# Twelve modulation tiles of layer 0 moved from VectorE row sums to TensorE, and the remaining row sums dealt out anew over the two down projections

## The chip, the cores and the metric

The kernel runs on one core of a Trainium2 chip. The metric is device time in microseconds (us) of one execution; the time given is the median of three. TensorE is PE in the rows, VectorE DVE, ScalarE ACT, GpSimd POOL; SyncE's queue (SP) issues most of the loads.

## The reference

Two layers of a diffusion backbone over 256 latent and 256 context tokens, width 1024. What matters here is the modulation: six vectors per layer are computed from the conditioning `c` and, for the context, from `c_ctx`, and they scale, shift and gate everything else.

```python
silu_c, silu_cc = silu(c), silu(c_ctx)
xc = ctx
for layer in range(2):
    mod   = silu_c  @ w_mod[layer] + b_mod[layer]      # 1024 -> 6 * 1024
    mod_c = silu_cc @ w_mod[layer] + b_mod[layer]
    sh1, sc1, g1, sh2, sc2, g2 = split(mod, 6)         # and the same for mod_c
    h, hc = rms_norm(x, n1) * (1 + sc1) + sh1, ...
    y, yc = mixer(h, hc)      # layer 0: neighbourhood attention + gated linear attention
    x  = x + g1 * y           # layer 1: retention, latent output only
    h2 = rms_norm(x, n2) * (1 + sc2) + sh2
    x  = x + g2 * conv_ffn(h2, up, down)
    ...                       # the context xc likewise, in layer 0
return rms_norm(x)
```

## The kernel before

All 512 tokens are held feature by feature (X, eight blocks of 128 features by 512 tokens). Every weight product is made of three fp32r products (helper `mm3`, lines 297 to 299): high part by high part, high by low, low by high. A weight piece of 128 x 1024 (a down projection's pieces are 768 and 640 wide) is loaded into one of the four slots of the ring `raw` (line 240, on SP's queue), copied rounded by ScalarE into `WH` (line 261), and the remainder is formed into `WL` by VectorE for a job's first piece (line 265) and by GpSimd for its second (line 263). `WH` and `WL` have four slots, two jobs' worth.

The work is a list of **jobs** (two output blocks of an up or input projection; one block of a down projection). `pieces` is the list of loads in the order of the jobs; piece n goes into raw slot n mod 4, and a slot is loaded again when the piece in it has been read. `before` puts extra pieces ahead of a job's weights. There are two kinds:

- **A modulation piece on TensorE** (`mods`, `use_mod`, lines 435 on, products at line 302): a quarter of the 1024 input features by 512 columns of `w_mod`. Eight small fp32 products, 128 x 128 by 128 x 32, each into a quarter of a PSUM bank; each shows as two records. Four pieces make one block of four tiles (128 modulation values each); the bank is held over the four, and the first of them is put off as long as no bank is to be had. Then `mod_post` transposes the bank on VectorE (line 467), adds the bias (478) and, for scales, makes `amod` (485).
- **A row sum on VectorE** (`row_sums`, `use_row`, line 453): one tile, 128 rows of 1024 weights, multiplied with the broadcast conditioning and summed along the row by one tensor_tensor_reduce; a second pass for the context where the tile needs it. Scales take one more small instruction per pass (459).

Blocks 0 to 3 (tiles 0 to 15) are computed on TensorE at the very start. In the mixer stage ("mix": two value jobs of the linear attention, six jobs of the neighbourhood attention, two gate jobs) the kernel before has twelve TensorE pieces (tiles 16 to 27) and twelve row sums (tiles 28 to 39, `ROWS0`, two passes each). The other 56 row sums (tiles 40 to 47 of layer 0 with two passes, then 48 tiles of layer 1, the first 16 of them with two passes) lie in the feed-forward part of layer 0: one per job from the third of the first 13 up jobs (stage up0), two per job in the eight jobs of the first down projection (down0a), two per job in the nine further up jobs (up0b), two per job and one at the last in six jobs of the second (down0b).

A row sum needs the broadcast conditioning `cb` in SBUF. `open_rows` (line 1446) passes it through Silu on ScalarE (1448); it is called ahead of the mixer stage (1491) and again, with a fresh load, ahead of the output projection (1532). The two buffers of the first call, 2048 and 512 columns, are held until the mixer's scope is closed.

Beside the jobs run side tasks that are advanced in turn: the linear attention (`gla_gen`, `gla_head`: scans on VectorE at lines 787 and 851, small fp32 products) and four `na_pair` tasks, which begin by taking 3072 columns of scratch. With the first `cb` buffers in place 648 columns are free until linear attention heads give up theirs.

The order on each engine is not the program's: the framework arranges the instructions by a plan of times (`_TC = {"schedule_with_timeline_sim": True}`), and each engine then runs its list strictly in that order. Stages as read from the profile: start to 58 us, mixer jobs and side tasks 58 to 284, output projection 284 to 332, up0 332 to 476, down0a 476 to 539, up0b 539 to 652, down0b and its tail 652 to 715, layer 1 from 715.

Of the kernel before, what the change touches and what calls it, by code (L numbers as in the profile page):

```python
# [47 lines left out]
HID1 = 13056  # L48
NA0 = 4 * 2560
ROWS0 = tuple(range(28, 40))  # L50
RAWS = 4
WSL = 4
GLA_PAUSE = 14
# [75 lines left out]
def kernel(ctx: ExitStack, tc: tile.TileContext, I: dict, out: bass.AP):  # L129
    nc = tc.nc  # L130
# [4 lines left out]
    X = const.tile([128, KT, N2], F32, name="x")  # L135
    raw = const.tile([128, RAWS, 1024], F32, name="raw")
    WH = const.tile([128, WSL, 1024], F32R, name="wh")
# [30 lines left out]
    def buf(n, high=False, where="m"):  # L168
        b = (small if where == "s" else scope[where]).get(n, high)
        assert b is not None, (n, where)  # L170
        return b
# [65 lines left out]
    def try_load(upto=10000):  # L237
        while st["load"] < min(upto, len(pieces)) and st["load"] - st["piece"] < RAWS:
            src = pieces[st["load"]][0]
            nc.sync.dma_start(raw[:, st["load"] % RAWS, 0:src.shape[1]], src)  # L240
            st["load"] += 1

    def prep_next():
# [3 lines left out]
        src, use, arg = pieces[i]  # L247
        if not use(raw[:, i % RAWS, 0:src.shape[1]], *arg):
            return False
# [390 lines left out]
    def before(src, use, *arg):  # L640

        k = len(jobs)
        aux.setdefault(k, []).append((src, lambda *a: st["cur"] >= k - 1 and use(*a), arg))

    m_todo = deque()
    r_todo = deque()

    def mods(n):
        for _ in range(min(n, len(m_todo))):
            layer, c, q = m_todo.popleft()  # L650
            before(I["w_mod"][layer, c, q // 2][:, 1024 * (q % 2):1024 * (q % 2) + 1024], use_mod, layer, c, q)

    def row_sums(n):
        for _ in range(min(n, len(r_todo))):
            i, layer, t, both = r_todo.popleft()
            before(I["w_row"][i], use_row, layer, t, both)
# [595 lines left out]
    if True:  # L1252
# [11 lines left out]
        def mark(name):  # L1264
            seg[name] = len(jobs)

        def win(i, run):
            return W(I["w_in"][i], 2048, run)
# [8 lines left out]


        mark("mix")
        m_todo.extend((0, c, q) for c in range(4, 10) if 4 * c not in ROWS0 for q in range(4))  # L1280
        r_todo.extend((i, *r) for i, r in enumerate(_row_tiles()))
        mix = [win(8, tm_run(post_tm("gv", 0, 0))), win(9, tm_run(post_tm("gv", 256, 1)))]
        for hf in range(2):
            mix.append(win(hf, fm_run(8, [2 * hf, 2 * hf + 1], h_all, 512, post_naq, 4)))
# [4 lines left out]
        for i, j in enumerate(mix):  # L1289
            if i == 2:  # L1290
                mark("na")
            if i == 8:
                mark("gr")
            mods(-(-(24 - len(ROWS0)) * (i + 1) // 10) + (24 - len(ROWS0)) * i // -10)
            row_sums(-(-len(ROWS0) * (i + 1) // 10) + len(ROWS0) * i // -10)
            ja(j)

        def o_rhs(kt):
# [30 lines left out]
            ja(up_job(0, i, 512, S_[1]))  # L1329
        mark("down0a")  # L1330
        for m in range(8):
            row_sums(2)
            ja(down_job(0, 0, m, fm_run(HALF, [m], hid_rhs(0, 0, 512), 512, resid_post(0, 5, None, True), 4)))
        mark("up0b")
        for i in range(13, NFF):
# [1 line left out]
            ja(up_job(0, i, 512, S_[1]))  # L1337
        mark("down0b")
        for m in range(6):
            row_sums(2 if m < 5 else 100)  # L1340
            ja(down_job(0, 1, m, fm_run(HALF, [m], hid_rhs(HALF, 0, 512), 512, resid_post(0, 5, S_[2], True), 4)))
        mark("down0t")
        jl_d = [down_job(0, 1, m, None) for m in (6, 7)]
# [61 lines left out]
        nc.scalar.activation(ccs[:, :, :], ccs[:, :, :], AF.Silu)  # L1405
        sqrt_next()
        st["cur"] = 0
        dump = buf(512, True)
        G["msk"] = buf(256)
        m0 = []  # L1410

# [34 lines left out]
        def open_rows(cb, dump):  # L1446
            with after_h():
                nc.scalar.activation(cb.ap, cb.ap, AF.Silu)
            G["cb"], G["dump"] = cb, dump
# [13 lines left out]
        with tc.manual_schedule(engines={mybir.EngineType.PE}):  # L1463
            mod_pair(0)
            load_mod(6)
            load_mod(7)
            nc.sync.dma_start(cst[:, 0:C_SEL], I["cst"][:, 0:C_SEL])
            nc.sync.dma_start(G["msk"].ap.bitcast(I32), I["msk"])
            with tc.issue_after(first_h(0)):
                assert prep_next()  # L1470
            with after_h():
                assert prep_next()
            first_h(1)
            with after_h():
                assert prep_next() and prep_next()
            for c in range(4):
                first_mm(c, range(5))
                if c < 3:
                    mod_pair(c + 1)
                    if c == 1:  # L1480
                        row_bufs = [buf(2048, True), dump]
                        nc.sync.dma_start(row_bufs[0].ap, I["cb"])
                    first_h(2 * c + 2)
                    first_h(2 * c + 3)
                first_mm(c, range(5, 8))
# [2 lines left out]
        piece_done(jgq, 2)  # L1488
        for i in range(4):
            posts.append((post_gqk("k2", None) if i < 2 else post_gqk("q2", 0.125))(i % 2, gb[i]))  # L1490
        open_rows(*row_bufs)
        small.next = 0
        G["ws1"] = buf(2048, where="s")
        G["gpk"] = Sub(G["ws1"], 0, 1280)
# [35 lines left out]
        row_bufs = [buf(2048, True), buf(512)]  # L1530
# [150 lines left out]
def _row_tiles():  # L1681

    return [(0, t, True) for t in ROWS0 + tuple(range(40, 48))] + [(1, t, t < 16) for t in range(48)]

# [141 lines left out]
```

## Time and profile before

| | us |
|---|---|
| Three executions | 1213.65, 1217.60, 1224.94 |
| Median | 1217.6 |
| Profiled execution, own time | 1224.02 |
| Its span in the profile | 1222.2 |
| TensorE busy | 1165.3 (95%) |
| VectorE busy | 819.5 (67%) |
| TensorE's mean granted clock | 0.977 of full |

Busy is the time in which an engine has an instruction in hand; a product at half clock counts as busy too. The granted clock has two levels here, 1.0 (2.4 GHz) and 0.5 (1.2 GHz), so that a stretch of length L with mean clock m had (1 - m) x L of full-speed time taken away.

### The profile page before, as it was taken

How to read it: one execution, taken by the hardware profiler on the slowest of the kernel's cores; microseconds unless marked ns; L12 is line 12 of the kernel's file. 1: busy time of each engine (PE TensorE's matmuls, PEld its weight loads, DVE VectorE, ACT ScalarE, POOL GpSimd, SP SyncE). 2: the span in 40 equal slices, each digit the busy share in tenths (PEclk: the TensorE clock that was granted, in tenths of full speed). 3: DMA queues.
4: the chain of work that ended last, by engine and by line, in shares of the span. 5: the costliest groups of instructions: out<-in, count | busy, mean ns of one | idle time of the engine just before them, and what ended most of it. 6: DMA issues, size and time to landing. Idle time of an engine off the chain costs nothing.

```text
span 1222.2 us, 19879 instructions
## 1 busy us (share of the span) xinstructions
PE 1165.3 (95%) x7846; PEld 1023.8 (84%) x7846; DVE 819.5 (67%) x1344; ACT 547.5 (45%) x933; POOL 462.6 (38%) x326
## 2 busy tenths in 40 slices
PE   4999999989999999989899999999999999999997
PEld 3677866767898888867688889889999999999996
DVE  4498886464498889966865256647977736877532
ACT  4452344264463443212344364534555546666542
POOL 2124234232432322121212339954643354443342
PEclk8999988999999999989999989999999999999998
DMA  9653554213334445677643323322223553655562
GB/s 371 234 180 125 184 172 153 86 52 108 104 119 149 143 149 176 208 253 251 228 150 106 109 92 121 105 71 85 70 70 128 183 190 127 210 181 180 153 182 91
DMA packets 52365, 184.79 MB, mean 151 GB/s; under 512 B 5824, under 2 KB 6208, under 8 KB 50736
## 3 DMA queue, kind: packets, MB, share of 16 engines
q1 hardware_dynamic: 50256, 175.20, 43.5%
q0 software_dynamic: 1728, 7.80, 1.9%
q8 instruction: 61, 1.00, 0.3%
q10 hardware_dynamic: 288, 0.52, 0.1%
q14 instruction: 32, 0.26, 0.1%
HBM read 182.46 MB, written 1.05 MB: 150 GB/s over the span
## 4 chain that ended last, share of the span: by engine, by line
PE 69%; DVE 14%; DMA 6%; POOL 5%; issue 3%; ACT 2%; SPq 0%; DVEq 0%; ACTq 0%; POOLq 0%
PE bank L297 20%; PE bank L299 20%; PE bank L298 20%; PE bank L302 9%; DVE space L453 5%; DMA raw<-in_w_row_dram 5%; DVE wl L265 2%; POOL wl L263 1%; DVE space_r L1055 1%; PE bank L983 1%; POOL space L1151 1%; POOL space L1152 1%; DMA x<-in_xT_dram 1%; DVE space L1023 1%; DVE amod L459 1%
## 5 line engine op out<-in xcount | busy, mean ns | idle before, releaser
L263 POOL TENSOR_TENSOR wl<-raw,wh 128x1024 fp32r<-128x1024 f32 (+1 forms) x124 | 284.9, 2297 | 563.5 <-ACT wh L261 553.1
L299 PE MATMUL bank<-hh,wl 128*128 128x256 f32 (+1 forms) x1200 | 402.8, 336 | 13.8 <-DVE wl L265 11.1
L297 PE MATMUL bank<-hh,wh 128*128 128x256 f32 (+1 forms) x1200 | 403.5, 337 | 8.6 <-DVE space L989 3.5
L298 PE MATMUL bank<-hl,wh 128*128 128x256 f32 (+1 forms) x1200 | 402.6, 336 | 5.1 <-DVE hl L547 5.1
L261 ACT CAST wh<-raw 128x1024 fp32r<-128x1024 f32 (+1 forms) x248 | 241.9, 978 | 256.5 <-PE bank L298 125.3
L299 PEld LDWEIGHTS bank<-hh,wl 128*128 128x128 f32 x1200 | 230.4, 192 | 39.1 <-DVE wl L265 12.8
L297 PEld LDWEIGHTS bank<-hh,wh 128*128 128x128 f32 x1200 | 230.7, 192 | 36.2 <-ACT hh L545 4.0
L298 PEld LDWEIGHTS bank<-hl,wh 128*128 128x128 f32 x1200 | 230.5, 192 | 29.1 <-DVE hl L547 6.0
L265 DVE TENSOR_TENSOR wl<-raw,wh 128x1024 fp32r<-128x1024 f32 (+1 forms) x124 | 153.2, 1235 | 101.6 <-ACT wh L261 99.2
L453 DVE CUSTOM_DVE_ANT_0 space<-raw,space,vec 128x1024 bf16<-128x1024 f32 x104 | 155.0, 1490 | 39.4 <-DMA raw<-in_w_row_dram 35.1
L299 PE MATMUL bank<-space_r,wl 128*128 128x256 f32 (+1 forms) x374 | 123.6, 330 | 1.0 <-DVE wl L265 1.0
L298 PE MATMUL bank<-space_r,wh 128*128 128x256 f32 (+1 forms) x374 | 122.9, 329 | 0.0
L297 PE MATMUL bank<-space_r,wh 128*128 128x256 f32 (+1 forms) x374 | 122.3, 327 | 0.0
L297 PE MATMUL bank<-wh,hh 128*128 128x256 f32 x384 | 109.8, 287 | 0.3 <-ACT wh L261 0.3
L299 PE MATMUL bank<-wh,hl 128*128 128x256 f32 x384 | 108.8, 284 | 0.0
L298 PE MATMUL bank<-wl,hh 128*128 128x256 f32 x384 | 108.7, 283 | 0.0
L299 PEld LDWEIGHTS bank<-space_r,wl 128*128 128x128 f32 x374 | 70.3, 188 | 8.4 <-DVE wl L265 1.7
L1023 DVE SCALAR_TENSOR_TENSOR space<-bank,vec,space 128x510 f32<-128x510 f32 (+1 forms) x88 | 53.6, 610 | 34.7 <-ACT space L1019 34.6
L297 PEld LDWEIGHTS bank<-space_r,wh 128*128 128x128 f32 x374 | 70.7, 189 | 7.3 <-issue 0.4
L298 PEld LDWEIGHTS bank<-space_r,wh 128*128 128x128 f32 x374 | 70.2, 188 | 7.4
L297 PEld LDWEIGHTS bank<-wh,hh 128*128 128x128 f32 x384 | 73.2, 191 | 2.9 <-issue 2.1
L298 PEld LDWEIGHTS bank<-wl,hh 128*128 128x128 f32 x384 | 73.4, 191 | 1.7 <-DVE space L683 0.8
(249 smaller groups left out, 1641.6 us busy)
## 6 DMA issues: line engine op xcount, KB each, us to landing
raw<-in_ffn_up_dram SPq DMA_DIRECT2D x88, 512.0 KB, 3.8
raw<-in_w_row_dram SPq DMA_DIRECT2D x68, 512.0 KB, 4.2
raw<-in_ret_in_dram SPq DMA_DIRECT2D x48, 512.0 KB, 3.6
raw<-in_w_in_dram SPq DMA_DIRECT2D x24, 512.0 KB, 4.7
raw<-in_ffn_down_dram SPq DMA_DIRECT2D x32, 384.0 KB, 3.2
raw<-in_ffn_down_dram SPq DMA_DIRECT2D x32, 320.0 KB, 2.9
space<-in_w_mod_dram SPq DMA_DIRECT2D x8, 1024.0 KB, 13.8
raw<-in_ret_out_dram SPq DMA_DIRECT2D x16, 512.0 KB, 3.8
```

Source lines behind the costliest of these rows:

```text
L261: nc.scalar.copy(WH[:, s, 0:n], src)
L263: nc.gpsimd.tensor_tensor(WL[:, s, 0:n], src, WH[:, s, 0:n].bitcast(F32), op=ALU.subtract)
L265: nc.vector.tensor_sub(WL[:, s, 0:n], src, WH[:, s, 0:n].bitcast(F32))
L297: nc.tensor.matmul(out_ap, lhsT=ah, rhs=bh, start=first, stop=False, skip_group_check=True)
L298: nc.tensor.matmul(out_ap, lhsT=ah, rhs=bl, start=False, stop=False, skip_group_check=True)
L299: st["pe"] = nc.tensor.matmul(out_ap, lhsT=al, rhs=bh, start=False, stop=last, skip_group_check=True).ins
L302: st["pe"] = nc.tensor.matmul(out_ap, lhsT=lhsT, rhs=rhs, start=start, stop=stop, skip_group_check=True).ins
L453: nc.vector.tensor_tensor_reduce(G["dump"].ap.bitcast(BF16), src, G["cb"].ap[:, 1024 * v:1024 * v + 1024], 1.0, vec[:, V_BMOD + 48 * layer ...
L459: nc.vector.scalar_tensor_tensor(out=amod[:, layer, s // 4, k, v:v + 1], in0=modt[:, layer, t, v:v + 1], scalar=1.0, in1=vec[:, g0:g0 + 1] ...
L983: nc.tensor.transpose(banks[bs[e]][:, u * 256 + qt * 128:u * 256 + qt * 128 + 128], gs[e][:, qt, u, :], ident)
L1023: nc.vector.scalar_tensor_tensor(out=yv[:, :, 1:256], in0=pv[:, :, 0:255], scalar=vec[:, w:w + 1], in1=yv[:, :, 1:256], op0=ALU.mult, op1= ...
L1055: nc.vector.tensor_sub(hl, yb.ap, hh.bitcast(F32))
```

## The change

The twelve row sums of the mixer stage are no longer made; blocks 7, 8 and 9 (tiles 28 to 39) join the TensorE pieces, 24 instead of 12 over the ten jobs, and the 24 extra loads of the stage stay 24, of 512 KB each. The first `open_rows`, its 1 MB load of `cb` and the two buffers fall away. The 56 other row sums stay, in the same order; in down0a there is one per job instead of two, in down0b three instead of two (and four instead of one at its sixth job). So eight row sums go from down0a to later jobs.

```diff
+SKIP = len(ROWS0)
...
-        m_todo.extend((0, c, q) for c in range(4, 10) if 4 * c not in ROWS0 for q in range(4))
-        r_todo.extend((i, *r) for i, r in enumerate(_row_tiles()))
+        m_todo.extend((0, c, q) for c in range(4, 10) for q in range(4))
+        r_todo.extend((i, *r) for i, r in enumerate(_row_tiles()) if i >= SKIP)
...
-            mods(-(-(24 - len(ROWS0)) * (i + 1) // 10) + (24 - len(ROWS0)) * i // -10)
-            row_sums(-(-len(ROWS0) * (i + 1) // 10) + len(ROWS0) * i // -10)
+            mods(24 * (i + 1) // 10 - 24 * i // 10)
...
         mark("down0a")
         for m in range(8):
-            row_sums(2)
+            row_sums(1)
...
         mark("down0b")
         for m in range(6):
-            row_sums(2 if m < 5 else 100)
+            row_sums(3 if m < 5 else 100)
...
-        dump = buf(512, True)
...
-                    if c == 1:
-                        row_bufs = [buf(2048, True), dump]
-                        nc.sync.dma_start(row_bufs[0].ap, I["cb"])
...
-        open_rows(*row_bufs)
```

## Rows read from the trace of the kernel before

**Rows 1.** The page's first part: busy time of each engine, share of the span, instructions.

```profile
PE 1165.3 (95%) x7846; PEld 1023.8 (84%) x7846; DVE 819.5 (67%) x1344; ACT 547.5 (45%) x933; POOL 462.6 (38%) x326
```

**Rows 2.** Busy time by stage: stretch, its length, then busy us (instructions) of PE, PEld, DVE, ACT and POOL, the granted clock, the DMA engines' share, GB/s.

```profile
58.00:190.00 132.00, 124.62 (x918) 96.54 (x916) 113.90 (x232) 53.60 (x104) 44.68 (x44) 0.95 0.49 162
190.00:284.00 94.00, 90.26 (x538) 67.59 (x536) 50.72 (x102) 41.13 (x95) 27.24 (x31) 0.95 0.25 83
...
476.00:539.00 63.00, 62.05 (x266) 49.43 (x266) 53.87 (x93) 13.40 (x18) 13.99 (x7) 1.00 0.69 216
539.00:652.00 113.00, 101.87 (x434) 82.47 (x433) 84.92 (x118) 39.02 (x52) 23.22 (x10) 0.97 0.61 202
652.00:715.00 63.00, 63.00 (x344) 53.25 (x344) 20.06 (x31) 22.32 (x31) 19.86 (x14) 1.00 0.33 101
```

**Rows 3.** The same view for line 453 alone (VectorE's row sums; each pass counts two instructions): stretch, length, DVE busy.

```profile
58.00:190.00 132.00, 33.86 (x48) 0.95 0.49 162
...
476.00:539.00 63.00, 33.90 (x50) 1.00 0.69 216
```

**Rows 4.** TensorE's timeline in the mixer stage, three rows at which it had waited for VectorE's scans: start us, us, instruction, and in brackets the idle time before it and what ended that.

```profile
92.17 0.66 PE L302 MATMUL bank<-cst,space 128*64 128x128 f32 x8 [1.24 <-DVE space L787]
...
114.42 0.50 PE L297 MATMUL bank<-hh,wh 128*128 128x512 f32 x1 [1.93 <-DVE x L851]
...
162.88 1.52 PE L302 MATMUL bank<-space_r 128*128 128x512 f32 x2 [1.95 <-DVE x L851]
```

**Rows 5.** The granted clock around five waits (columns as in rows 2).

```profile
112.00:120.00 8.00, 6.07 (x35) 4.24 (x34) 6.96 (x19) 0.89 (x2) 4.87 (x3) 0.79 0.15 38
160.00:174.00 14.00, 12.05 (x58) 7.60 (x57) 12.62 (x37) 1.78 (x5) 2.88 (x1) 0.63 0.59 189
187.00:198.00 11.00, 9.25 (x48) 6.68 (x48) 6.51 (x14) 4.42 (x14) 2.94 (x5) 0.69 0.75 236
258.00:266.00 8.00, 4.48 (x13) 3.53 (x13) 4.95 (x7) 6.24 (x18) 2.87 (x3) 0.79 0.42 131
539.00:550.00 11.00, 7.03 (x21) 5.29 (x20) 8.39 (x11) 2.10 (x2) 2.36 (x1) 0.69 0.72 236
```

**Rows 6.** TensorE's timeline in down0a and up0b: the rows at which it had waited for a weight's remainder.

```profile
531.88 0.50 PE L299 MATMUL bank<-space_r,wl 128*128 128x512 f32 x1 [0.95 <-DVE wl L265]
...
543.82 0.80 PE L299 MATMUL bank<-hh,wl 128*128 128x512 f32 x1 [3.97 <-DVE wl L265]
...
580.46 0.50 PE L299 MATMUL bank<-hh,wl 128*128 128x512 f32 x1 [1.47 <-DVE wl L265]
...
594.56 0.50 PE L299 MATMUL bank<-hh,wl 128*128 128x512 f32 x1 [2.93 <-DVE wl L265]
...
608.45 0.50 PE L299 MATMUL bank<-hh,wl 128*128 128x512 f32 x1 [2.71 <-DVE wl L265]
```

**Rows 7.** What that queue waited for between 476 and 620 us: total us, times, longest.

```profile
SPq L240 <- DVE modt L453: 62.6, 35, 4.3
SPq L240 <- DMA raw<-in_w_row_dram: 21.7, 15, 3.5
```

**Rows 8.** The queue that issues the loads, in a stretch of up0b: start us, us (of the group), load, count.

```profile
580.43 0.33 SPq L240 DMA_DIRECT2D raw<-in_ffn_up_dram  x1
585.18 2.26 SPq L240 DMA_DIRECT2D raw<-in_w_row_dram  x2
587.53 0.38 SPq L240 DMA_DIRECT2D raw<-in_ffn_up_dram  x1
589.89 3.23 SPq L240 DMA_DIRECT2D raw<-in_w_row_dram  x2
594.53 0.33 SPq L240 DMA_DIRECT2D raw<-in_ffn_up_dram  x1
```

**Rows 9.** The chain of waits ahead of 58 us, where two modulation pieces (x16) lie between products of 512 columns: start us, us.

```profile
44.11 0.57 PE bank L302 x16
44.68 0.43 PE bank L297
45.12 0.57 PE bank L302 x16
45.69 0.43 PE bank L298
46.12 0.23 PE bank L299
```

**Rows 10.** TensorE's timeline: a modulation piece on TensorE at which it waited, and the wait just before it.

```profile
189.42 0.66 PE L983 MATMUL bank<-cst,space 128*128 128x128 f32 x4 [1.53 <-DVE space_r L724]
...
190.41 1.08 PE L302 MATMUL bank<-raw,ccs 128*32 128x128 f32 x16 [0.22 <-DMA raw<-in_w_mod_dram]
```

**Rows 11.** Groups by line and shape: busy us, mean ns of one, idle before.

```profile
L453 DVE CUSTOM_DVE_ANT_0 space<-raw,space,vec 128x1024 bf16<-128x1024 f32 x104 | 155.0, 1490 | 39.4 <-DMA raw<-in_w_row_dram 35.1 <-ACT space L1448 3.8
```

**Rows 12.** One VectorE instruction of each `mod_post`: times in ns (least, median, most).

```profile
L467 DVE STREAM_TRANSPOSE small<-bank x7: 313/317/318, 19.3 to 191.6; 128x128 f32<-128x128 f32 x7
```

**Rows 13.** TensorE's timeline: the third long wait of the mixer stage.

```profile
261.55 0.52 PE L297 MATMUL bank<-hh,wh 128*128 128x512 f32 x1 [3.52 <-DVE space L989]
```

**Rows 14.** ScalarE's timeline: the first call of `open_rows`, a table load and the Silu.

```profile
54.91 1.28 ACT L1448 ACT_TABLE_LOAD   x1
56.20 1.92 ACT L1448 ACTIVATE space<-space 128x2048 f32<-128x2048 f32 x1
```

## The prediction

> **What bounds the kernel now.** I read the page's first part, then busy time by stage, then what TensorE had waited for, and last the queue that issues the loads. TensorE is busy 95% of the span [rows 1]: work added to it costs its full length unless it fills a hole, and what a faster VectorE can give is only the holes that TensorE leaves and the half-clock time behind them. By stage [rows 2] the holes sit in three places: 7.4 us in the mixer stage at 58 to 190 (132.00 less 124.62), 3.7 us at 190 to 284, and 1.0 and 11.1 us in down0a and up0b.
>
> In 58 to 190 VectorE is as full as TensorE, 113.90 of 132 us, and 33.86 of these are row sums [rows 2, 3]. TensorE's long waits there end on VectorE's scans of the linear attention: 1.24, 1.93 and 1.95 us, together 5.1 [rows 4]. Each scan step is short and stands in VectorE's strict order among row sums. Behind two of these waits the clock falls to its lower level, 1.2 GHz: a mean of 0.79 over 8 us and 0.63 over 14 us, so 1.7 and 5.2 us are lost [rows 5].
>
> In down0a and up0b all five waits end on a weight's remainder formed on VectorE: 0.95, 3.97, 1.47, 2.93 and 2.71 us, 12.0 in all [rows 6], and the 3.97 is followed by 11 us at 0.69, 3.4 us lost [rows 5]. VectorE isn't full in up0b (84.92 of 113 us), so this is order, not amount. The loading queue waited 62.6 us, 35 times, for row sums to be read out of their slots, more than for anything else [rows 7]. With two row sums and two weight pieces to a job, four slots repeat job by job: row sums always get the same two slots, run ahead in these, and weights have the other two. The queue is in order, so it shows one weight piece, two row tiles, one weight piece, 7.1 us from weight to weight (580.43, 587.53, 594.53) [rows 8]; an up job here takes 11.3 us (101.87 busy over nine jobs) and needs one per 5.7 us. The reserve in `WH` and `WL` is used up by 540, and TensorE then goes at the loads' pace.
>
> **The change part by part.** Against the profiled execution's own 1224.0 us (span 1222.2):
>
> 1. Twelve more modulation pieces on TensorE: one takes 0.57 us between products, and the next 512-column product takes 0.43 us where the one after it takes 0.23 [rows 9]. So 0.77 us a piece, 12 x 0.77 = +9.2. Two pieces back to back share that restart: 12 x 0.57 = 6.8 is the low end. At the lower clock a piece takes 1.08 [rows 10]: 13.0 is the high end. I take 9.2, since pieces between large products are the row's own case.
>
> That restart is also the place for a rule that speaks against the change: the Trainium skill, TensorEngine Tiling (Array Packing), section Key Properties, says that a change of tiling mode drains the array, and these pieces use a quarter of its columns. The row above agrees with it by 0.20 us a piece. Counted without the drain the sum would be 2.4 us lower, with it as it stands here.
>
> 2. Twelve row sums of two passes leave VectorE: 24 of 1.49 us on average [rows 11], 35.8 us, in place of which three `mod_post` cost 0.32 us each for the transpose [rows 12] and less for each of their few adds. VectorE goes from 113.90 to about 80 of 132 us, so the scans should come in time: the 5.1 us of waits and the 1.7 + 5.2 behind them go, -12.0. Low end: none goes, if the scans' own chain is what is late. What is late next: the 1.53 and 3.52 us around 188 and 260 [rows 10, 13] with 3.4 and 1.7 of clock [rows 5], 10.2 in all. They end on copies and transposes of the neighbourhood attention after the row sums are done. I leave them as they are; if the pairs start earlier because 3208 instead of 648 scratch columns are free, up to -10.2.
>
> 3. The first `open_rows` goes: 1.28 + 1.92 us of ScalarE [rows 14] and 1 MB of loads. TensorE is busy without a hole in the 22 us that follow, so I cost it at nothing; if it did uncover something, at most its own 3.2.
>
> 4. The loads of the mixer stage stay 24 beside the weights, but the 12 new pieces are read by TensorE and not VectorE, and a late one stops TensorE's whole list: side products, main products and all who wait for them. The one late piece of before waited 0.22 us behind a 1.53 us hole [rows 10]. Cost 0 taken; the other end is a rival below. That the first piece of a block waits for a bank now happens six times instead of three, and the weights stand behind it in the list; a bank is held nearly throughout in both, so 0 as well.
>
> 5. Down0a with one row sum a job has three pieces a job: the rhythm of the slots is broken, row sums can't run ahead, and eight of them (about 17 us of VectorE, 33.90 for 16 [rows 3]) are gone before up0b begins. The waits 0.95 and 3.97 and the clock behind the latter go: -8.3.
>
> 6. Up0b keeps two and two, and so the pace of 7.1 us a weight piece while row sums run ahead. But only its own 18 and two more can run ahead now; in down0b three a job end the rhythm, where before the eleven of down0b could too. Nine such steps fall behind by 9 x 1.4 = 12.6 us, against a reserve of one job, 11.3. By that 7.1 us (1.47 + 2.93 + 2.71) would shrink to 1.3; I take half of them, -3.6, since the reserve may not be full; ends 0 and -7.1.
>
> 7. Down0b has 19 row sums and 12 weight pieces in six jobs of 7.8 us (62.05 busy over eight). At up0b's pace, 7.1 us for three pieces, 31 take 73 us against 47 and a reserve of two jobs, 16: 10 us late. At down0a's, 32 pieces in 63 us with 0.95 of waiting [rows 2, 6], they take 61 us and are not late. The nearer is down0a, the same jobs and widths, and these row sums have one pass: +1.5, ends 0 and 10. VectorE covers it with 20.06 of 63 us busy there [rows 2].
>
> Sum: +9.2 - 12.0 = -2.8 in the mixer stage, -8.3 - 3.6 + 1.5 = -10.4 behind it, together -13.2: 1224.0 - 13.2 = 1210.8. The profiled execution lies 6.4 above the median of the three shown, and the three are 11 us apart, which is of the size of these waits; as far as they differ by waits that go, the changed kernel won't have the difference. I take off half of it, 3.2: **1207.6 us**, 0.8% under the median of 1217.6.
>
> **The rivals.**
>
> - *More goes than I count.* The waits at 188 and 260 with their clock (10.2) and the other half of up0b's (3.5) go as well: 1193.9. For it: all five holes follow VectorE or its neighbours. Against: no row sum lies near 260.
> - *The mixer stage gives nothing back.* TensorE's list holds the scans' products at places where other waits, on ScalarE and POOL, take over; the pieces are a plain addition, and +9.2 - 10.4 leaves 1222.8, less 3.2: 1219.6. For it: TensorE is busy for 124.62 of the 132 us anyway [rows 2]. Against: all three long waits name the scans.
> - *Up0b and down0a stay as late as they are.* The rhythm of two and two is unchanged where four of the five waits end (up0b): -2.8 + 1.5 leaves 1222.7, less 3.2: 1219.5. Against: the reserve was used up in down0a already, where the 0.95 shows it.
> - *Slower: the load wait moves from VectorE to TensorE.* Place: the mixer stage, a modulation piece whose slot was freed late, in front of everything else on TensorE. Price: 1.75 us of hole (1.53 + 0.22) and 3.4 of half clock behind it [rows 5, 10], 5.2 each. From three such pieces of the 24 on my 13.2 are gone; with five, +12.8, less 3.2: 1233.6. For it: VectorE waited 35.1 us for row tiles in the whole run [rows 11], and these pieces use the same slots and queue. Against: in before only one of twelve was late.
>
> **How the numbers follow.** Forecast 0.42, own range 1200 to 1215; more goes 0.17; mixer gives nothing 0.13; the feed-forward waits stay 0.12; slower 0.16. Within 1% (12.2 us, about what a measurement of this kernel can tell from no change) means 1205.4 to 1229.8. Faster: all of the first rival and some 0.18 of the forecast, 0.35. Slower: nearly all of the last, 0.15. The rest, 0.50, is within. The range that leaves out 0.2, most of the slower case and the far end of the first rival, is 1192 to 1224.
>
> **What would show each step.** Of the mixer stage: no TensorE wait on lines 787 and 851 over 1 us between 58 and 190, full clock at 112 to 120 and 160 to 174, and VectorE near 80 of 132 us; 24 pieces of 0.57 us each. Wrong if TensorE's waits there end on modulation loads, or if the output projection begins later than 284. Of the rest: no wait over 1 us at the start of up0b and full clock there, waits of a few us at most in the rest of up0b, row tiles still being loaded in down0b, and no wait there over 2 us. Wrong if TensorE waits for remainders in down0b, or if the queue shows weight pieces 7 us apart before up0b.

## The result and the profile after

The changed kernel takes 1205.65 us (median of seven executions, 1203.85 to 1209.57) where the kernel before takes 1217.60 (seven, 1213.65 to 1224.94). The ratio is 0.9892, with a 95% interval of 0.9861 to 0.9923: 1.1% faster. The profiled execution of the changed kernel took 1209.57 us, with a span of 1207.8; that is 14.5 less than the profiled one of before, and it is the slowest of its seven. The forecast was 1207.6. In what follows, helper lines after line 51 are one higher than before (453 is 454, 297 to 299 are 298 to 300).

The total came out close, its parts did not. Stage borders are read from TensorE's timeline: the last product of the norm's statistics ahead of up0, the first product of each later part, the norm's statistics again ahead of layer 1, and the last group of products. Lengths in us, from the profiled executions:

| stretch | before | after | difference | forecast |
|---|---|---|---|---|
| start to up0 (mixer and output projection) | 332.3 | 320.9 | -11.4 | -2.8 |
| up0 | 144.0 | 144.0 | 0.0 | 0 |
| down0a | 63.0 | 61.6 | -1.4 | with up0b |
| up0b | 112.8 | 99.8 | -13.0 | with down0a -11.9 |
| down0b and its tail | 64.9 | 78.7 | +13.8 | +1.5 |
| layer 1 | 497.7 | 495.5 | -2.2 | 0 |

So the new dealing over the two down projections gave 14.4 us and took 13.8 back; the gain is the mixer's. In layer 1 nothing was changed: its 2.2 us are what two executions differ by. The page's first part of the kernel after (busy time of each engine), and busy time by stage (columns as in [rows 2]: stretch, length, then PE, PEld, DVE, ACT and POOL busy with their counts, granted clock, DMA share, GB/s):

```profile
PE 1157.7 (96%) x8038; PEld 1018.4 (84%) x8038; DVE 793.7 (66%) x1293; ACT 541.7 (45%) x930; POOL 455.8 (38%) x326
```

```profile
58.00:190.00 132.00, 127.77 (x1060) 98.13 (x1058) 85.01 (x182) 57.00 (x120) 45.47 (x51) 1.00 0.43 141
190.00:284.00 94.00, 91.20 (x601) 69.98 (x598) 49.61 (x103) 40.23 (x83) 25.25 (x26) 0.98 0.35 120
464.90:526.50 61.60, 61.60 (x265) 49.57 (x264) 42.52 (x68) 13.22 (x17) 13.92 (x8) 1.00 0.49 166
526.50:626.30 99.80, 98.56 (x433) 80.98 (x432) 77.99 (x110) 36.84 (x49) 20.61 (x9) 1.00 0.59 197
626.30:705.00 78.70, 69.12 (x351) 56.31 (x349) 46.10 (x72) 24.68 (x35) 21.75 (x17) 0.93 0.56 185
```

In the mixer stage VectorE has gone from 113.90 [rows 2] to 85.01 of 132 us (forecast: near 80), and the clock from 0.95 to 1.00. Down0a and up0b run almost without a hole, and down0b, which was clean before, has 9.6 us of holes and a clock of 0.93.

TensorE's timeline of the kernel after (start, length, instruction; in brackets the idle time before it and what ended that): three of its waits ahead of the output projection, the only one over 0.5 us in up0b, then those over 0.5 us in down0b.

```profile
60.69 1.09 PE L303 MATMUL bank<-hh,small 128*32 128x512 f32 x8 [2.02 <-DMA small<-in_gpk_dram]
...
110.78 1.13 PE L303 MATMUL bank<-space,x 128*128 128x128 f32 x8 [1.00 <-DVE small L852]
...
252.76 0.65 PE L303 MATMUL bank<-space 128*64 128x256 f32 x2 [2.18 <-DVE space L990]
...
582.47 0.50 PE L300 MATMUL bank<-hh,wl 128*128 128x512 f32 x1 [0.92 <-DVE wl L266]
...
635.26 0.50 PE L298 MATMUL bank<-space_r,wh 128*128 128x512 f32 x1 [2.45 <-ACT space_r L1055]
638.04 0.79 PE L299 MATMUL bank<-space_r,wh 128*128 128x512 f32 x1 [2.28 <-DVE space_r L1056]
644.95 0.50 PE L298 MATMUL bank<-space_r,wh 128*128 128x512 f32 x1 [1.16 <-ACT space_r L1055]
660.65 0.51 PE L298 MATMUL bank<-space_r,wh 128*128 128x512 f32 x1 [1.97 <-ACT wh L262]
...
662.10 0.50 PE L300 MATMUL bank<-space_r,wl 128*128 128x512 f32 x1 [0.72 <-DVE wl L266]
```

The waits of [rows 4] are down to 1.00 and less, that at 188 [rows 10] is gone, and that of [rows 13] has shrunk from 3.52 to 2.18. New is the 2.02 us at 60.69 for a small load of other weights. The granted clock around these places (columns as above), to be held against [rows 5]:

```profile
112.00:120.00 8.00, 8.00 (x75) 6.32 (x74) 5.86 (x22) 4.74 (x17) 2.44 (x7) 1.00 0.59 195
160.00:174.00 14.00, 14.00 (x86) 9.55 (x84) 9.65 (x31) 7.71 (x23) 2.60 (x5) 1.00 0.37 114
187.00:198.00 11.00, 11.00 (x69) 8.12 (x68) 4.05 (x6) 3.42 (x7) 5.50 (x7) 1.00 0.82 276
247.00:258.00 11.00, 8.47 (x50) 5.27 (x52) 8.19 (x10) 4.95 (x9) 3.02 (x3) 0.84 0.29 97
526.00:537.00 11.00, 11.00 (x50) 9.05 (x49) 10.90 (x21) 3.13 (x4) 2.48 (x1) 1.00 0.57 199
634.00:648.00 14.00, 9.19 (x27) 6.52 (x28) 12.18 (x20) 4.43 (x7) 1.53 (x1) 0.76 0.62 199
```

The first three stretches, of the mixer stage, and the start of up0b are back at the upper level; that of the attention pairs, at 247, is as slow as before. The one at 634 is new: 0.76 over 14 us is 3.4 us lost.

What went on in down0b is told by VectorE's timeline between TensorE's last up product (626.1) and its wait at 638.04. L454 is a row sum; L1024, L1026 and L1047 are the convolution and the gate of a hidden block, L1056 (after ScalarE's L1055) its lower part.

```profile
628.07 1.28 DVE L454 CUSTOM_DVE_ANT_0 space<-raw,space,vec 128x1024 bf16<-128x1024 f32 x1 [0.97 <-DMA raw<-in_w_row_dram]
...
629.28 0.74 DVE L1024 SCALAR_TENSOR_TENSOR space<-bank,vec,space 128x510 f32<-128x510 f32 x1
...
630.01 1.28 DVE L454 CUSTOM_DVE_ANT_0 space<-raw,space,vec 128x1024 bf16<-128x1024 f32 x1
...
631.21 0.74 DVE L1026 SCALAR_TENSOR_TENSOR space<-bank,vec,space 128x510 f32<-128x510 f32 x1
...
632.65 1.29 DVE L454 CUSTOM_DVE_ANT_0 space<-raw,space,vec 128x1024 bf16<-128x1024 f32 x1 [0.63 <-DMA raw<-in_w_row_dram]
...
633.86 0.69 DVE L1047 TENSOR_TENSOR space<-space 128x512 f32<-128x512 f32 x1
...
636.07 1.92 DVE L1056 TENSOR_TENSOR space_r<-space,space_r 128x512 fp32r<-128x512 f32 x1
```

L1024, L1026 and L1047 each stand behind a row sum in VectorE's strict order: three row sums of 1.28 us, and 0.97 and 0.63 us of waiting for the tiles of two of them, 5.4 us in all. TensorE's 2.45 us at 635.26 end on ScalarE's L1055, which had waited for the L1047 at 633.86. Its 2.28 at 638.04 end on the L1056 at 636.07, and no row sum stands directly ahead of that one: VectorE first makes a weight's remainder and another L1024, and the L1056 then takes 1.92 us, with a remainder on GpSimd beside it. The two rows, of ScalarE's and GpSimd's timelines:

```profile
634.59 0.62 ACT L1055 CAST space_r<-space 128x512 fp32r<-128x512 f32 x1 [2.88 <-DVE space L1047]
...
635.91 1.53 POOL L264 TENSOR_TENSOR wl<-raw,wh 128x640 fp32r<-128x640 f32 x1 [9.36 <-ACT wh L262]
```

Over the three FFN stretches from down0a on VectorE stood 37.1 us in front of row sums whose tile had not landed, 9.9 of them in down0b; in the kernel before it was 24.3, and none of it in down0b. Line 453 alone in the kernel before (stretch, length, DVE busy with its count; two instructions a pass), down0a, up0b and down0b:

```profile
476.30:539.30 63.00, 33.81 (x51) 1.00 0.69 218
539.30:652.10 112.80, 33.78 (x48) 0.97 0.61 202
652.10:717.00 64.90, 0.00 (x0) 1.00 0.35 105
```

and line 454 after:

```profile
464.90:526.50 61.60, 21.05 (x31) 1.00 0.49 166
526.50:626.30 99.80, 30.79 (x46) 1.00 0.59 197
626.30:705.00 78.70, 19.89 (x28) 0.93 0.56 185
```

The kernel before deals eleven row sums to down0b, but they had all run ahead: none was left when it began. After, fourteen of the nineteen dealt to it fall into it (one pass each).

### The profile page after: what moved, and what is told of

Its sections match the earlier page's. It is cut to its first block, busy times and chain, and to the rows that moved or that the text cites. A ratio compares the mean times of both kernels' runs of the same rounds, so it can differ in the third digit from the quotient of the medians.

```text
span 1207.8 us, 20237 instructions
## 1 busy us (share of the span) xinstructions
PE 1157.7 (96%) x8038; PEld 1018.4 (84%) x8038; DVE 793.7 (66%) x1293; ACT 541.7 (45%) x930; POOL 455.8 (38%) x326
## 3 DMA queue, kind: packets, MB, share of 16 engines
HBM read 181.41 MB, written 1.05 MB: 151 GB/s over the span
## 4 chain that ended last, share of the span: by engine, by line
PE 73%; DVE 10%; DMA 7%; POOL 4%; issue 3%; ACT 2%; SPq 0%; DVEq 0%; POOLq 0%; ACTq 0%
PE bank L298 20%; PE bank L299 20%; PE bank L300 20%; PE bank L303 12%; DMA raw<-in_w_row_dram 5%; DVE space L454 3%; DVE wl L266 2%; ACT wh L262 1%; PE bank L984 1%; POOL wl L264 1%; DVE space L1026 1%; DMA x<-in_xT_dram 1%; DMA small<-in_gpk_dram 1%; DVE space L1024 0%; DMA raw<-in_ffn_up_dram 0%
## 5 line engine op out<-in xcount | busy, mean ns | idle before, releaser
L264 POOL TENSOR_TENSOR wl<-raw,wh 128x1024 fp32r<-128x1024 f32 (+1 forms) x124 | 279.4, 2253 | 563.5 <-ACT wh L262 534.5
L266 DVE TENSOR_TENSOR wl<-raw,wh 128x1024 fp32r<-128x1024 f32 (+1 forms) x124 | 157.7, 1272 | 107.5 <-ACT wh L262 105.7
L454 DVE CUSTOM_DVE_ANT_0 space<-raw,space,vec 128x1024 bf16<-128x1024 f32 x80 | 121.3, 1516 | 44.8 <-DMA raw<-in_w_row_dram 44.3
L298 PE MATMUL bank<-space_r,wh 128*128 128x256 f32 (+1 forms) x374 | 124.5, 333 | 5.6 <-ACT space_r L1055 3.6
L299 PE MATMUL bank<-space_r,wh 128*128 128x256 f32 (+1 forms) x374 | 124.7, 334 | 2.4 <-DVE space_r L1056 2.3
L298 PEld LDWEIGHTS bank<-space_r,wh 128*128 128x128 f32 x374 | 71.5, 191 | 14.4 <-ACT space_r L1055 4.5
L1024 DVE SCALAR_TENSOR_TENSOR space<-bank,vec,space 128x510 f32<-128x510 f32 (+1 forms) x88 | 53.6, 609 | 33.1 <-ACT space L1020 33.0
## 6 DMA issues: line engine op xcount, KB each, us to landing
space<-in_w_mod_dram SPq DMA_DIRECT2D x8, 1024.0 KB, 14.2
```

The lines of the kernel that those rows point to most:

```text
L264: nc.gpsimd.tensor_tensor(WL[:, s, 0:n], src, WH[:, s, 0:n].bitcast(F32), op=ALU.subtract)
L266: nc.vector.tensor_sub(WL[:, s, 0:n], src, WH[:, s, 0:n].bitcast(F32))
L298: nc.tensor.matmul(out_ap, lhsT=ah, rhs=bh, start=first, stop=False, skip_group_check=True)
L299: nc.tensor.matmul(out_ap, lhsT=ah, rhs=bl, start=False, stop=False, skip_group_check=True)
L454: nc.vector.tensor_tensor_reduce(G["dump"].ap.bitcast(BF16), src, G["cb"].ap[:, 1024 * v:1024 * v + 1024], 1.0, vec[:, V_BMOD + 48 * layer ...
L1024: nc.vector.scalar_tensor_tensor(out=yv[:, :, 1:256], in0=pv[:, :, 0:255], scalar=vec[:, w:w + 1], in1=yv[:, :, 1:256], op0=ALU.mult, op1= ...
```

## Experiments

Ten kernels, in three groups that each shared their runs of the kernel before (medians 1217.57, 1217.94 and 1219.65). "Mark" is the beginning of up0 as in the table above; it comes from one profiled execution of each kernel. Five of the kernels have the mixer stage of the changed kernel, and their marks lie at 319.7, 320.4, 320.9, 322.6 and 323.8; the two that have that of before, at 332.3 and 329.4. So a difference between two marks is known to 3 or 4 us, whatever its decimals.

**The change in halves.** First the mixer half alone (the changed kernel with the old dealing):

```diff
         for m in range(8):
-            row_sums(1)
+            row_sums(2)
...
-            row_sums(3 if m < 5 else 100)
+            row_sums(2 if m < 5 else 100)
```

> The mixer half of the change alone: 24 modulation pieces on TensorE, no first open_rows, and the row sums of the feed-forward dealt as in the kernel before (two a job in both down projections). Theory (the gain is the mixer stage's, the new dealing moves time from up0b to down0b and nets about nothing): the step to the second half of layer 0 comes about 11 us earlier, waits for weight remainders at the start of and within up0b as before (about 12 us), no long waits in down0b; 1204 to 1208 us, within 3 us of the changed kernel. Rival (as predicted, most of the gain lies in the new dealing): 1213 to 1216.

1209.56 us, ratio 0.9931 (0.9903 to 0.9959). Mark 319.7; down0a 62.9, up0b 109.4, down0b 64.9, so the FFN is that of before but for 3.4 us in up0b, where the waits for remainders, with the one at the end of down0a, are 8.4 us in all (12.0 before). The total lies between what the two sides expected, nearer to the theory. Then the dealing half alone (the same two lines changed in the kernel before, the other way):

> The new dealing alone: mixer stage as in the kernel before, one row sum a job in down0a, three in down0b. Theory: up0b about 13 us shorter, down0b about 14 longer, 1214 to 1219 us, no change that can be told from the kernel before. Rival (the dealing is worth the 10.4 us that were predicted): 1205 to 1209.

1217.76 us, ratio 0.9998 (0.9976 to 1.0020): nothing. Mark 329.4; down0a 61.6, up0b 100.8, down0b 79.1: the same giving and taking back as in the full change, -13.4 and +14.2 against before. The first two waits of [rows 6] are gone here too. Where the gain is, is thereby shown: 8.0 us in the medians for the mixer half, nothing for the dealing. Whether the full change (12.0) is better than its mixer half is not: the medians are 4 us apart with overlapping intervals, and the profiled executions stand the other way round (1205.28 for the half, 1209.57 for the whole).

**No row sums in the FFN.** The 56 row sums are left out, the modulation values they would have made are taken as 1.

```diff
-            before(I["w_row"][i], use_row, layer, t, both)
+            mod_ready.add((layer, t))
...
```

> The changed kernel without the 56 row sums of the feed-forward and their loads (those modulation values are a constant 1 instead): what row sums still cost. Theory (the waits in up0b and down0b all come from row sums in VectorE's and the loading queue's order): down0a 61.5, up0b about 98 to 100, down0b about 64 us without waits over 1 us or half clock, so 14 to 17 us under the changed kernel, 1189 to 1192. Rival (the last up jobs' chains are late by themselves): waits of several us at the start of down0b stay, 1198 or more.

1195.58 us, ratio 0.9815 (0.9777 to 0.9853), between the two sides. Up0 to the end of down0b takes 368.4 us instead of 384.1, 15.7 less, without one wait of TensorE over 0.5 us between up0's first product and layer 1; up0b is 98.0 and down0b 64.9. Those are the floors for this stretch, as the theory had them. The median is only 10 below the changed kernel's: the mark of this kernel lies at 322.6, 1.7 later, and layer 1 took 1.3 longer, though no work was changed in either.

**The scratch of the first open_rows.** Its buffers, load and Silu put back, with nothing to use them:

```diff
+        dump = buf(512, True)
...
+                    if c == 1:
+                        row_bufs = [buf(2048, True), dump]
+                        nc.sync.dma_start(row_bufs[0].ap, I["cb"])
...
+        open_rows(*row_bufs)
```

> The changed kernel with the first open_rows put back (1 MB load, Silu on ScalarE, both buffers held through the mixer stage) though no row sum uses it there. Theory (the mixer stage gains because VectorE is relieved of the row sums): 0 to 3 us above the changed kernel, the output projection begins within 3 us of it, long clock loss does not come back. Rival (it gains because 3208 instead of 648 scratch columns let the attention pairs begin early): 6 to 10 us above it, with waits around 188 and 260 back.

1210.38 us, ratio 0.9946 (0.9920 to 0.9972); mark 325.9, 5.0 later than the changed kernel's, between what the two sides expected. Where the changed kernel waits 0.61 and then 2.18 us, this one waits for an attention pair's scaling:

```profile
247.24 0.33 PE L984 MATMUL bank<-cst,space 128*128 128x128 f32 x1 [3.14 <-DVE space L974]
```

To tell the columns from the load and the Silu, the 2560 columns alone were held:

```diff
+        dump = buf(512, True)
...
+                    if c == 1:
+                        row_bufs = [buf(2048, True), dump]
```

> The changed kernel with the two buffers of the first open_rows (2560 columns) reserved through the mixer stage, but without its load and its Silu. The kernel that had all three was 4.7 us above the changed one. Theory (scratch: the first attention pair has to wait for a linear attention head's columns): 3 to 6 us above the changed kernel, 1209 to 1212, the output projection's end 4 to 6 us later. Rival (the Silu with its table load on ScalarE and the 1 MB load): within 1.5 us of the changed kernel, 1204 to 1207.

1210.58 us, ratio 0.9949 (0.9929 to 0.9968); mark 325.2. Load and Silu cost nothing that shows, as the forecast's third step had it; the columns cost 4.9 us in the medians, and that was not in the sum. The mark says 4.3, of which the spread of marks leaves little: 323.8 was reached with the columns free.

**What the twelve pieces cost.** Left out, with the scratch free; tiles 28 to 39 are taken as 1.

```diff
-        m_todo.extend((0, c, q) for c in range(4, 10) for q in range(4))
+        m_todo.extend((0, c, q) for c in range(4, 7) for q in range(4))
...
-            mods(24 * (i + 1) // 10 - 24 * i // 10)
+            mods(-(-12 * (i + 1) // 10) + 12 * i // -10)
...
```

> The changed kernel with only the first twelve modulation pieces of the mixer stage; tiles 28 to 39 are left out (a constant 1 instead), no row sums there either. It prices the twelve added pieces. At 0.57 us each, restarts hidden: 6.8 us under the changed kernel, 1198 to 1200. At 0.77 us: 9.2 under it, 1195 to 1198. If half of them lie in holes that TensorE has anyway: 2 to 5 under it.

Mark 312.5, 8.4 before the changed kernel's: 0.70 us a piece, between the forecast's 0.57 and 0.77 (7.2 to 11.3, or 0.60 to 0.94 a piece, against the five marks). In the median only 2.4 of it shows (1203.30, 1200.53 to 1214.52, ratio 0.9898, 0.9859 to 0.9938), with down0b 1.5 longer.

**Other rhythms in the feed-forward part.** The mixer half alone, with row sums dealt one and three in turn in down0a and up0b, so that the slots' rhythm breaks without fewer row sums:

```diff
-            row_sums(1)
+            row_sums(3 if m % 2 else 1)
...
-            row_sums(2)
+            row_sums(2 if i == 13 else 3 if i % 2 else 1)
...
-            row_sums(3 if m < 5 else 100)
+            row_sums(2 if m < 5 else 100)
```

(against the changed kernel; the first line is down0a's, the second up0b's, the third down0b's).

> The new mixer stage with 16 row sums in down0a and 18 in up0b as in the mods-only kernel (1209.6 us), but alternately one and three a job instead of two and two, so that row sums do not always meet the same two slots; down0b as before, two a job. Theory (with two and two the row sums run ahead in their own two slots and the queue's order starves the weights): up0b about 100 us instead of 109, waits for remainders there under 3 us in all, down0b a few us longer as its row sums stay there, 1200 to 1205. Rival (only the number of row sums in a stage counts, not their rhythm): within 2 us of 1209.6, up0b 107 to 111.

1218.61 us, ratio 1.0006 (0.9976 to 1.0037). Up0b shrank from 109.4 to 104.5, with 1.05 us of waits for remainders left, so the rhythm has a part in them; and down0b grew from 64.9 to 80.6: six tiles no longer ran ahead, and their row sums stood among the last hidden blocks. Its three waits there:

```profile
645.65 0.64 PE L298 MATMUL bank<-space_r,wh 128*128 128x512 f32 x1 [3.85 <-ACT space_r L1055]
650.01 0.80 PE L299 MATMUL bank<-space_r,wh 128*128 128x512 f32 x1 [3.72 <-DVE space_r L1056]
656.86 0.80 PE L298 MATMUL bank<-space_r,wh 128*128 128x512 f32 x1 [2.65 <-ACT space_r L1055]
```

Two row sums about its start take 3.45 and 2.59 us instead of 1.28, each with a remainder on GpSimd beside it. Neither side expected that total. It shows what the forecast had not seen: running ahead is bought with weights in up0b and pays in down0b.

**Fewer row sums.** Tiles 40 to 47 go to TensorE as well, 32 pieces in the mixer stage, and 48 row sums are left.

```diff
-SKIP = len(ROWS0)
+SKIP = len(ROWS0) + 8
...
-        m_todo.extend((0, c, q) for c in range(4, 10) for q in range(4))
+        m_todo.extend((0, c, q) for c in range(4, 12) for q in range(4))
...
-            mods(24 * (i + 1) // 10 - 24 * i // 10)
+            mods(32 * (i + 1) // 10 - 32 * i // 10)
...
-            row_sums(1 if i > 1 else 0)
+            row_sums(1)
...
-            row_sums(3 if m < 5 else 100)
+            row_sums(1 + m % 2 if m < 5 else 100)
...
```

> The changed kernel, in which also tiles 40 to 47 of layer 0 (two passes each) go to TensorE, 32 pieces in the mixer stage; the 48 tiles of layer 1 are dealt one a job in up0 and down0a, two in up0b, one and two alternately in down0b, nine there instead of 19. Theory (down0b's waits come from row sums among the last up jobs' chains, a piece costs 0.6 to 0.8 us): mixer stage 5 to 6 us longer, down0b 66 to 70 instead of 78.7 us, 1198 to 1204. Rival (nine row sums there wait as long as 19, since each stops VectorE behind a load): down0b 75 or more, 1209 to 1213.

1201.53 us (1200.09 to 1203.10), ratio 0.9869 (0.9840 to 0.9899), the fastest that leaves nothing out. Its interval overlaps that of the changed kernel. Eight pieces more and a wait of 1.88 us at the head of up0 cost 9 us (mark 325.6, up0 148.3); then down0a 61.6, up0b 98.0 and down0b 64.9 are the floors of the kernel without any row sums. Five passes still fall into down0b, and they do no harm; all five come after the last block's L1047 (636.42):

```profile
535.50:633.50 98.00, 98.00 (x434) 81.12 (x433) 73.18 (x102) 39.15 (x53) 21.71 (x9) 1.00 0.56 188
633.50:698.30 64.80, 63.87 (x353) 53.96 (x351) 25.10 (x40) 21.76 (x32) 21.94 (x16) 1.00 0.43 138
```

That is busy time by stage again, up0b and down0b. Whether it is the smaller number of row sums or their place, this run does not tell apart.

**VectorE's load in the mixer stage.** The twelve tiles made both ways: the changed kernel with the first `open_rows` of above and its row sums too.

```diff
-        r_todo.extend((i, *r) for i, r in enumerate(_row_tiles()) if i >= SKIP)
+        r_todo.extend((i, *r) for i, r in enumerate(_row_tiles()))
...
             mods(24 * (i + 1) // 10 - 24 * i // 10)
+            row_sums(-(-12 * (i + 1) // 10) + 12 * i // -10)
```

> The changed kernel with the twelve row sums of the mixer stage (and the first open_rows, its load and its 2560 scratch columns) made as well, beside the 24 pieces on TensorE: the same twelve tiles are computed twice, so nothing is left out. It is the changed kernel's FFN dealing and the scratch of e4, with only VectorE's row sums put back. Compared with e4_hold_bufs (last norm product ahead of the second half of layer 0 at 325.9 us; 1210.4), the difference is the row sums on VectorE (and twelve more loads in the stage). Theory (the row sums' load on VectorE is what made TensorE wait, whatever TensorE itself has to do): the scan waits come back at over 1 us each with half clock behind them, and the mark moves to 337 to 343, which is 11 to 17 later than e4's, for 1221 to 1228. Rival (pieces on TensorE give the scans the time that the row sums take: with twelve more pieces TensorE is later anyway and the row sums hide beside them): 326 to 332, 1210 to 1217. Rival (the queue: 36 instead of 24 loads beside the weights make TensorE wait for modulation or weight pieces): mark over 343, and the waits end on loads, not on lines 787 and 851.

1235.94 us, ratio 1.0130 (1.0091 to 1.0169); mark 343.8, 17.9 later than with the scratch alone (the medians are 25.6 apart, with 5.9 more in the FFN). The rival by which the row sums hide beside a later TensorE is out. The price is above what the theory gave (11 to 17), and the queue has a share in it, since one wait ends on a modulation piece:

```profile
87.73 0.44 PE L303 MATMUL bank<-cst,space 128*64 128x128 f32 x4 [1.37 <-DVE space L788]
...
113.62 0.80 PE L298 MATMUL bank<-hh,wh 128*128 128x512 f32 x1 [5.47 <-DVE x L868]
...
168.78 1.16 PE L303 MATMUL bank<-space,x 128*128 128x128 f32 x8 [2.84 <-POOL x L873]
...
215.81 1.08 PE L303 MATMUL bank<-raw,ccs 128*32 128x128 f32 x16 [1.62 <-DMA raw<-in_w_mod_dram]
```

Lines 788 to 873 are the linear attention's scans and heads: 9.7 us of these waits end on them, 1.6 on the queue. From 56 us to the mark TensorE's idle time is 19.8 us (9.8 with the scratch alone) and its clock 0.96 (0.99).

**Row sums kept out of the head of down0b.**

```diff
-            row_sums(3 if m < 5 else 100)
+            row_sums((0, 0, 5, 5, 5, 100)[m])
```

> The changed kernel with the 19 row sums of the second down projection dealt 0, 0, 5, 5, 5, 4 over its six jobs instead of 3, 3, 3, 3, 3, 4; nothing is left out. Theory (the 13.8 us that this projection gained come from row sums that stand ahead of the last hidden blocks' chain on VectorE and wait there for their loads): none is dealt near those blocks now, so the waits of TensorE on hidden blocks at its start (2.45, 2.28 and 1.16 us in the changed kernel) shrink under 1 us and the projection goes from 78.7 to 65 to 70 us; total 1195 to 1200. Rival (row sums and weights share the slots and the queue: five tiles ahead of a weight piece make the piece late): the waits move to the later jobs and end on weights or their remainders, 6 to 12 us with half clock behind; the projection stays at 75 to 82 and the total at 1203 to 1210.

1212.38 us, ratio 0.9925 (0.9893 to 0.9957). Down0b takes 82.3: the rival, and worse than it said.

```profile
636.99 0.79 PE L298 MATMUL bank<-space_r,wh 128*128 128x512 f32 x1 [4.21 <-ACT space_r L1055]
...
668.63 0.79 PE L298 MATMUL bank<-space_r,wh 128*128 128x512 f32 x1 [6.30 <-ACT wh L262]
```

The 6.30 is the weight behind five tiles, as the rival had it. The 4.21 shows that the wait on the hidden block did not go either. Which job a row sum is dealt to sets its load's place in the queue, and it did not keep row sums away from the last hidden blocks: VectorE's timeline of this kernel, just before that wait.

```profile
625.72 1.28 DVE L454 CUSTOM_DVE_ANT_0 space<-raw,space,vec 128x1024 bf16<-128x1024 f32 x1 [3.28 <-DMA raw<-in_w_row_dram]
...
632.83 1.28 DVE L454 CUSTOM_DVE_ANT_0 space<-raw,space,vec 128x1024 bf16<-128x1024 f32 x1 [2.89 <-DMA raw<-in_w_row_dram]
634.04 0.08 DVE L454 DVE_READ_ACCUMULATOR2_ANT modt<- 128x1 f32 x1
634.04 0.74 DVE L1024 SCALAR_TENSOR_TENSOR space<-bank,vec,space 128x510 f32<-128x510 f32 x1
```

VectorE stands 2.89 us before a row sum whose tile is not there, with the hidden block's L1024 right behind it.

## Why the prediction was right in total and wrong in its parts

*Step 1, the pieces (+9.2): right.* Leaving them out moves the mark by 8.4, and the rows bear out the price taken. TensorE's timeline of the kernel after:

```profile
131.00 0.39 PE L300 MATMUL bank<-hh,wl 128*128 128x512 f32 x1
131.32 0.64 PE L303 MATMUL bank<-raw,ccs 128*32 128x128 f32 x16
131.89 0.50 PE L298 MATMUL bank<-hh,wh 128*128 128x512 f32 x1
132.23 0.40 PE L299 MATMUL bank<-hl,wh 128*128 128x512 f32 x1
132.47 0.40 PE L300 MATMUL bank<-hh,wl 128*128 128x512 f32 x1
```

From one start to the next the product ahead of the piece takes 0.32, the piece 0.57, the product behind it 0.34, the next 0.24; without a piece large products start 0.23 apart. So the piece costs 0.77, as forecast. [rows 9] goes by the ends of products and puts the restart of 0.20 behind the piece; by their starts half of it lies ahead. The Trainium skill (TensorEngine Tiling (Array Packing), Key Properties) states that a change of tiling mode drains the array. This trace agrees, with about 0.10 us at each of the piece's two changes.

*Step 2, the waits in the mixer stage (-12.0): the failed term of this half, by size.* The scan waits and the clock behind them went, as forecast, but for 1.8 us (0.84 at 93.61 and 1.00 at 110.78). What the step left as it was went in part too: the wait before 188 with its clock, 1.75 + 3.4, and 0.7 of those near 260. By rows that is -16.1; with the new 2.0 at 60.69 and the pieces' 8.4 it is -5.7 of the -11.4 measured. The other 5.7 lie in TensorE's busy time, in no wait and in no slow stretch that I can point to, and stay open by rows; 2.9 is what two executions of the stage of before differ by. By experiments, in the mark: the row sums on VectorE and their loads -17.9 (the tiles made both ways against the scratch alone), the scratch -5.0, the pieces +8.4, together -14.5; that is 3 more than the -11.4, within what marks are known to. The scratch, 4.7 and 4.9 us in the medians, was a missing term: the forecast named the columns, with up to -10.2, and took nothing. Its reason against, that no row sum lies near 260, asked after the wrong resource; holding the columns brings a wait of 3.14 us on an attention pair there.

*Steps 3 and 4 (0 and 0): right.* Load and Silu cost nothing that shows. No piece of the changed kernel waited for its load (the 2.02 us at 60.69 are another's), so the rival on the slower side had no case; with 36 extra loads in the stage instead of 24 one such wait appears, 1.62 us.

*Steps 5 and 6 (-8.3 and -3.6): right in sum.* -14.4 measured, of which -1.4 in down0a. The waits 0.95 and 3.97 and the clock behind are gone, and of the 7.1 us in the rest of up0b 0.92 is left; the 1.3 that step 6's own working left over was the better value than the half taken.

*Step 7, down0b (+1.5): the step that failed.* It measured +13.8, beyond its own upper end of 10, and by another mechanism. The step asked whether weight loads come at pace, and covered the row sums with VectorE's free time, "20.06 of 63 us busy". VectorE had the time: 46.10 of 78.7 us. But it is in strict order, and a row sum holds up the hidden block behind it by its own 1.28 us and by its wait for its tile (3.84 and 1.6 us ahead of the first of the waits), and TensorE waits for the block: 8.7 us of holes (9.6 less the 0.9 at its last border, which before had as well) and 5.1 more of busy time at the lower clock (0.07 x 78.7 is 5.5), which is the 13.8. Of the holes 5.9 us end on hidden blocks (1.2 of that is the L1056 that GpSimd slows), and 2.7 on a weight and its remainder, the part that the step had asked about. Two of the waits break the step's own sign, no wait over 2 us in down0b. Step 6 had it that the eleven row sums of down0b could run ahead before. All of them did (line 453 has none in that stretch), so that row sums among these hidden blocks were new, and step 7 did not draw that.

*The total and the chances.* Two errors of 9 and 12 us with opposite signs left 1207.6 near 1205.65, and that is luck. The 3.2 taken off for the spread came out at 2.5: the profiled execution lies 3.9 above its median, that of before 6.4. "More goes" was right on the wait at 188, worth 5 us, and on the rest of up0b, 2.5 more than was taken, and wrong near 260. "The mixer stage gives nothing back" and "the feed-forward waits stay" fell.

## What to carry to other kernels

On an engine in strict order, free time is no cover: ask of each instruction added to it how long it takes, what it waits for and who stands behind it. Here, where extra loads share a ring with weights, running ahead cost weights in one stage and spared the next, and dealing them out differently moved the price or raised it; with some taken away (48 row sums instead of 56) it was gone. Columns of scratch that a removed part gives back are a term of the sum: find the task that is waiting for them. And compare marks of several executions before reading one to the tenth.

## What was not expected of the hardware

Some waits cost nearly their own length a second time, in the clock. With the tiles made both ways TensorE idled 10.0 us more ahead of the mark than with the scratch alone (19.8 against 9.8), and the mark moved by 17.9; the other 8 us are at the lower level (0.04 x 287.8 = 11.5 us lost against 0.01 x 269.9 = 2.7). In down0b of the changed kernel it was 8.7 of holes and 5.1 of clock. That is no fixed price: from 56 us to the mark the mixer half alone idled 7.7 us, and the kernel with the late row sums 9.1, with the clock at 1.00 throughout.

Two kinds of VectorE instruction took longer beside GpSimd. From 315 to 730 us of the changed kernel the 17 L1056 with no GpSimd instruction beside them took 0.68 to 0.69 us, the five with one 1.78 to 2.74; a row sum took 1.28 alone and up to 3.39 beside one.
